# Soft-routed experts on one core: the last set of weight sums cut in two halves, and the first product's additions at other places

## The chip, the cores and the metric

The kernel runs on one core of a Trainium2 chip. The metric is the device time of one execution in microseconds; the median of three runs is given, and one further execution was taken with the hardware profiler. TensorE (PE) multiplies, VectorE (DVE) and ScalarE (ACT) compute, GpSimd (POOL), SyncE (SP) and ACT issue DMAs, each from an ordered queue of its own.

## The reference

Every token passes through all eight experts, and the results are added with the softmax of the router's logits as weights. There are 16 × 512 tokens of 512 values, eight matrices of 512 × 2048, and the output is 8192 × 2048 in float32.

```python
logits_max = np.max(router_logits, axis=-1, keepdims=True)
probs = np.exp(router_logits - logits_max)
probs = probs / np.sum(probs, axis=-1, keepdims=True)
output = np.zeros((batch, seq, expert_hidden), dtype=np.float32)
for e in range(n_experts):
    expert_out = np.matmul(x, expert_weights[e])
    output += probs[:, :, e:e+1] * expert_out
```

## The kernel before, in words

Since the weight of an expert is a factor per token, the sum over experts is one large matrix product: the tokens' rows, scaled by each expert's probability and set side by side, times the eight expert matrices set on top of each other. The kernel computes it by a scheme of Strassen and Winograd with seven products for eight, twice nested. The outer seven are called P1 to P7. The blocks of the left side are two expert halves by the even and odd 256-token blocks; a number q from 0 to 15 names a pair of such blocks ("row pair"). The blocks of the right side are two expert halves by two column halves, called 11, 12, 21 and 22, 22 being the lower right one. The output blocks are C11 and so on.

Inside a product of one row pair there are again seven steps, each of eight matmuls of 128 × 512 into one PSUM bank. Such a step is a "slot", and the kernel's own clock puts it at 1.73 us (`SLOT`). Most stages hold two row pairs and thus 14 slots. The stages run in this order: P1 (0 to 6), P2 (7 to 14), P5 and P6 mixed (15 to 31, where `k5` = 15 is the first and `k6` = 31 the last), P7 and P4 in turn (32 to 47, `k7` = 32; P7 is in the even stages, P4 in the odd ones), and P3 (48 to 56, `k3` = 48). P4 and P3 take their first steps in thirds (`by_thirds`), so their pieces are smaller.

The order of the program is written by hand. `at(stage, slot, make)` hangs an action on a slot, and `slots_after(stage, slot, n)` counts n slots on across stages. DVE's work that isn't tied to a matmul goes into a queue by `later(cost, make)`, and `slack()` takes tasks from it whenever the kernel's own clock has DVE ahead of PE. `flush(task)` empties that queue up to a task. All subtractions and additions on DVE are issued by `tt` (line 110), all DMAs of POOL by `pool` (line 124), those of SP by `sp` (line 121), whole weight blocks by ACT in `fetch_w` (line 167), and all matmuls by `mm` (line 133).

The buffers that matter here: `w`, 15 weight blocks of 1 MB; `h`, 12 places of 256 KB for results on their way to the output ("result places"), where also the rows that a product is added onto are fetched (`h<-kept`, rows of P1 put aside in DRAM, and `h<-out_dram`, rows of the output written earlier); `u`, one single buffer of 512 KB, for a temporary left side, for weight pieces, and in P4's stages for four small sums (`room_u`). A place is used again when the program's semaphores say that its last reader, often a DMA, is done.

The right sides of P4 and P3 are differences of weight blocks, and they are made while earlier products run. P4's are made in quarters (`by_parts`: first quarter at stage 17, slot 4, then every 38 slots). P3's are made in eighths by `by_eighths`: an eighth loads four pieces of 128 KB of block 22 (`u<-wd`), makes four differences in place on DVE through `sums_in_place`, and stores each (`wd<-u`). Before it begins it flushes the last eighth's tasks. All eight were hung at stage 17, slot 8 + 17j. From stage 46 on, ACT fetches the finished blocks for P3, 1 MB each (`turnover`).

P1 is needed in several output blocks. For ten of the row pairs it is added to C11 by DMAs of POOL that accumulate from DRAM to DRAM (`add_kept`, `out_dram<-kept` in the profile): four of 256 KB for each pair, forty in all. They were hung from stage 35 on, one every four slots.

At stage 28 ACT loads pieces into `u` for P7's first difference (`ahead_part`).

Of the kernel before, what the change touches and what calls it, by code (L numbers as in the profile page):

```python
# [31 lines left out]
def kernel(  # L32
# [8 lines left out]
    P = 128  # L41
    f16 = mybir.dt.float16
# [7 lines left out]
    C = H // P  # L50
    HE = E // 2
    NB = 512
# [24 lines left out]
    def h_tile(shape, dtype):  # L77
        return hpool.tile(shape, dtype, name="h", tag="h")
# [19 lines left out]
    def note(i):  # L98
        last[i.ins.engine] = i.ins
        if ordered[0]:  # L100
            tc.keep_in_program_order(i)
# [21 lines left out]
    def pool(o, i, **how):  # L123
        note(nc.gpsimd.dma_start(out=o, in_=i, **how))  # L124
# [15 lines left out]
    def new_u():  # L140
        return zpool.tile([P, K8, HQ], f16, name="u", tag="u", bufs=1)
# [18 lines left out]
    def kept_w(what, kn):  # L160
        if (what, kn) not in stored:
            stored[what, kn] = dram.tile([P, K8, NB], f16, name="wd")
        return stored[what, kn]
# [209 lines left out]
    def flush(task):  # L373
        while task is not None and not task.done:
            queue.popleft().run()
# [340 lines left out]
    def at(stage, slot, make):  # L716
        hooks.setdefault((stage, slot), []).append(make)

    def add(*products):
        stages.append(products)  # L720
        return len(stages) - 1
# [43 lines left out]
    def product(r, q, **how):  # L765
        left, loads = left_of(r, q)
        lefts[r, q] = left
        p = None
        if r == 1:
            def sink(tn, o):  # L770
                pool(kept_rows(q)(tn), o)
            p = Product(right[1], left, sink)
        elif r == 2:
            if q >= ON_BASE or q in WITH_KEPT:
                bases[2, q] = Base(kept_rows(q))
            p = Product(right[2], left, to_out(q, 0, 0), bases.get((2, q)))
        elif r == 5:
            bases[6, q] = m1 = Base(kept_rows(q))
            m1.task = {}

            p = Product(right[5], left, to_out(q, 1, 0))
        elif r == 6:
            m1 = bases[6, q]

            def base(tn):
                need(m1.task[tn])
                return m1.t[tn]
            p = Product(right[6], left, to_out(q, 0, 1), base)
        elif r == 7:
            base = products[6, q].o.__getitem__  # L790
            if q < KEPT_Z:
                base = bases[7, q] = Base(lambda tn: out_rows(q, 0, 1, tn))
            p = Product(right[7], left, to_out(q, 1, 1), base)
        elif r == 4:
            p = Product(right[4], left, to_out(q, 1, 0, accum_op=ADD), products[7, q].o.__getitem__)
        else:
            p = Product(right[3], left, to_out(q, 0, 1, accum_op=ADD), **how)
        p.loads = loads
        products[r, q] = p
        return p  # L800
# [198 lines left out]
    k5 = add(product(5, 0), product(5, 1))  # L999
# [5 lines left out]
    k7 = k6 + 1  # L1005
# [4 lines left out]
    k3 = add(product(3, 0))  # L1010
    for q in ((1, 2), (3, 14), *zip(range(4, 14, 2), range(5, 14, 2))):
        add(*(product(3, i) for i in q))
    end = add(product(3, 15))
# [28 lines left out]
    for n, q in enumerate(ORDER_7[1:], 1):  # L1042
        stage = k7 + 2 * n
# [71 lines left out]
    for i, (kn, e) in enumerate((kn, e) for kn in (ODD, (0, 0), (1, 1), (1, 0)) for e in range(2)):  # L1115
        stage = ND + i - 2 if kn != ODD else 2 + 2 * i
# [4 lines left out]
    ORDER = ((0, 0), (0, 1), (1, 1), (1, 0))  # L1121
# [13 lines left out]
    def sums_in_place(part, b, r, cost):  # L1135

        def one(p, o, x, y):
            def make():
                tt(o, x, y, SUB)
                part(p, o)  # L1140
            return later(cost, make)
        one(5, b[0, 0], b[0, 1], b[0, 0])
        one(7, b[0, 1], b[1, 1], b[0, 1])
        one(6, b[1, 1], b[1, 1], b[0, 0])
        return one(4, b[1, 0], b[1, 0], b[1, 1])
# [13 lines left out]
    def slots_after(stage, slot, n):  # L1159
        slot += n  # L1160
        while slot >= 7 * len(stages[stage]):
            slot -= 7 * len(stages[stage])
            stage += 1
        return stage, slot

    def part_of(what, kn, chunks):
        return kept_w(what, kn)[:, chunks, :]
# [3 lines left out]
    def by_parts(stage, slot, every, r, load, between, when):  # L1171

        for j in range(4):
            b, chunks = {}, ds(2 * j, 2)

            def begin(b=b, j=j, chunks=chunks):
                flush(last_part[0])
                t = new_w()
                for i, kn in enumerate(ORDER):
                    b[kn] = t[:, ds(2 * i, 2), :]  # L1180
                    load(b[kn], kn, j, chunks)

            def go_on(b=b, chunks=chunks):
                for kn in b:
                    if kn != ODD:
                        between(b[kn], kn, chunks)

            def end(b=b, chunks=chunks):
                last_part[0] = sums_in_place(lambda p, o: pool(part_of((r, p), (0, 0), chunks), o), b, r, 0.69)
            at(*slots_after(stage, slot, j * every), begin)  # L1190
            if between is not None:
                at(*slots_after(stage, slot, j * every + when[0]), go_on)
            at(*slots_after(stage, slot, j * every + when[-1]), end)

    last_eighth = [None]

    def by_eighths(stage, slot, j):

        b, chunk = {}, ds(j, 1)

        def begin():
            flush(last_eighth[0])
            t = new_u().rearrange("p (i two) t -> p i (two t)", two=2)
            for i, kn in enumerate(ORDER):
                b[kn] = t[:, ds(i, 1), :]
                pool(b[kn], part_of("b22", kn, chunk))

        def end():
            last_eighth[0] = sums_in_place(lambda p, o: pool(part_of((3, p), (0, 0), chunk), o), b, 3, 0.42)
        at(*slots_after(stage, slot, 0), begin)  # L1210
        at(*slots_after(stage, slot, 9), end)

    def cast_part(q):
        def load(t, kn, j, chunks):
# [17 lines left out]
        later(0.69, make)  # L1232

    by_parts(k5 + 2, 4, 38, 4, load_p4, less_t2, (9, 20))
    for j in range(2 * C):
        by_eighths(k5 + 2, 8 + 17 * j, j)


    RAW = {1: (0, 0), 2: (1, 0), 3: (1, 1)}
# [99 lines left out]
    def add_kept(q, n, t):  # L1339
        pool(out_f[ds(2 * q * HQ + t * HP, HP), ds(n * NB, NB)], kept[q][n, ds(t * HP, HP), :], accum_op=ADD)  # L1340

    for n, q in enumerate(q for q in range(ON_BASE) if q not in WITH_KEPT):
        for i in range(4):
            at(*slots_after(k7 + 3, 0, 16 * n + 4 * i), lambda q=q, i=i: add_kept(q, i // 2, i % 2))

    finish = products[3, 15]
    finish.base = Base(lambda tn: out_rows(15, 0, 1, tn))
# [90 lines left out]
```

## Time and profile before

| what | us |
|---|---|
| median of 3 runs | 1383.88 |
| lowest and highest | 1382.93, 1389.23 |
| the profiled execution | 1386.03 |
| its span on the core | 1384.3 |
| mean granted TensorE clock in it | 0.991 of full speed |

In the profile's rows, a line such as "518.84 4.97 PE L133 MATMUL ps<-w,z ... x16 [3.96 <-DVE h L110]" reads: at 518.84 us after the span's start a run of 16 matmuls of line 133 began, which took 4.97 us; ahead of it PE was idle for 3.96 us, and what came last was DVE's work on a tile `h` at line 110. Tiles go by their names in the program without numbers; `wd` are blocks of weights in DRAM, `ps` and `pt` banks of PSUM, `z`, `d` and `u` left sides. "POOLq" and "SPq" are the DMA issues of these engines. In a table of DMA issues the last column is the median time from issue to landing.

### The profile page before, as it was taken

The page shows a single profiled execution, that of the slowest core. Times are in us where ns is not written, and L with a number is a line of the kernel's source. Part 1 is how long each engine was busy: PE and PEld are TensorE (multiplying, and loading weights), DVE is VectorE, ACT ScalarE, POOL GpSimd, SP SyncE. Part 2 cuts the span into 40 slices and gives each one's busy share as a digit, 9 for nine tenths or more (in the row PEclk, how much of TensorE's full clock was granted, in tenths as well). Part 3 has the DMA queues.
Part 4 walks back from the last instruction along what each step waited for, and adds up shares of the span by engine and source line. Part 5 has one row for each costly group of instructions (what it writes and reads, how often), then busy time and mean ns, then how long its engine had stood idle before and what let it go on. Part 6 is the DMA issues. An engine that isn't in the chain of part 4 may idle for free.

```text
span 1384.3 us, 19408 instructions
## 1 busy us (share of the span) xinstructions
PE 1353.9 (98%) x7062; PEld 689.7 (50%) x7062; DVE 1156.1 (84%) x1474; ACT 274.1 (20%) x573; POOL 437.1 (32%) x683
## 2 busy tenths in 40 slices
PE   9999999999999989999898999999999999899998
PEld 4556655555544434444343444554555455456554
DVE  7878898888898878878668789889888987898886
ACT  3233332222211111111101100110110011133331
POOL 3223332233233254435321212333433341223232
PEclk9999999999999999999998999999999999999999
DMA  9899979998999999999999888899999999999986
GB/s 184 245 213 249 274 220 254 297 286 260 305 302 275 279 293 309 289 310 301 274 266 315 291 303 198 203 250 200 261 261 217 230 254 320 314 282 230 218 128 121
DMA packets 187601, 355.71 MB, mean 257 GB/s; under 512 B 53104, under 2 KB 82032, under 8 KB 182640
## 3 DMA queue, kind: packets, MB, share of 16 engines
q0 software_dynamic: 88032, 185.12, 58.4%
q1 hardware_dynamic: 95728, 144.05, 34.8%
q10 hardware_dynamic: 3744, 25.30, 5.2%
q8 instruction: 55, 0.90, 0.3%
q14 instruction: 42, 0.34, 0.1%
HBM read 210.53 MB, written 176.36 MB: 279 GB/s over the span
## 4 chain that ended last, share of the span: by engine, by line
PE 41%; issue 7%; DMA 5%; POOL 1%; DVE 0%; POOLq 0%; ACT 0%; DVEq 0%
PE ps L133 32%; PE pt L133 8%; DMA out_dram<-h 2%; POOL out_dram L124 1%; DMA wd<-w 1%; DMA xs<-in_x_dram 1%; DMA wd<-u 1%; DVE h L110 0%; POOL u L124 0%; DVE ps L110 0%; DVE z L110 0%; DVE w L110 0%; POOL xs L124 0%; POOLq L124 0%; ACT h L1375 0%
## 5 line engine op out<-in xcount | busy, mean ns | idle before, releaser
L133 PE MATMUL ps<-w,z 128*128 128x512 f16 (+1 forms) x3784 | 823.6, 374 | 19.7 <-DVE h L110 13.1
L133 PEld LDWEIGHTS <-z 128*128 128x128 f16 x5256 | 515.1, 98 | 570.2 <-issue 23.3
L124 POOL DMA_DIRECT2D out_dram<-h x380 | 250.9, 667 | 650.2 <-ACT h L674 229.2
L133 PE MATMUL pt<-w,z 128*128 128x512 f16 (+1 forms) x1444 | 286.3, 343 | 0.0
L110 DVE TENSOR_TENSOR h<-ps,h 128x512 f32<-128x512 f32 x298 | 202.6, 687 | 73.1 <-PE ps L133 53.3
L110 DVE TENSOR_TENSOR z<-xT,pT 128x2048 f16<-128x2048 f16 x192 | 232.0, 1218 | 0.8 <-DMA xT<-xs 0.8
L133 PE MATMUL ps<-w,d 128*128 128x512 f16 x880 | 202.4, 382 | 4.4 <-DVE ps L110 4.4
L661 ACT COPY h<-ps 128x512 f32<-128x512 f32 x102 | 59.9, 587 | 400.3 <-PE ps L133 363.3
L133 PEld LDWEIGHTS <-d 128*128 128x128 f16 x880 | 86.7, 99 | 104.1 <-issue 8.3
L110 DVE TENSOR_TENSOR z<-z,d 128x2048 f16<-128x2048 f16 x110 | 131.9, 1218 | 0.0
L110 DVE TENSOR_TENSOR w<-w 128x1024 f16<-128x1024 f16 (+2 forms) x98 | 105.9, 1100 | 7.5 <-DMA wd<-w 5.9
L674 ACT COPY h<-ps 128x512 f32<-128x512 f32 x54 | 31.7, 587 | 283.0 <-PE ps L133 259.8
L110 DVE TENSOR_TENSOR h<-pt,h 128x512 f32<-128x512 f32 x95 | 64.9, 687 | 24.3 <-PE pt L133 22.2
L110 DVE TENSOR_TENSOR h<-h 128x512 f32<-128x512 f32 (+2 forms) x69 | 45.3, 678 | 36.4 <-DMA h<-kept 33.1
L110 DVE TENSOR_TENSOR d<-z 128x1024 f16<-128x1024 f16 x110 | 73.5, 685 | 0.7
L110 DVE TENSOR_TENSOR ps<-ps,h 128x256 f32<-128x256 f32 (+1 forms) x84 | 50.4, 603 | 19.4 <-PE ps L133 14.8
L657 ACT COPY h<-ps 128x512 f32<-128x512 f32 x89 | 49.9, 599 | 76.6 <-PE ps L133 55.7
L124 POOL DMA_DIRECT2D kept<-h x56 | 30.6, 548 | 87.6 <-DVE h L110 48.2
L110 DVE TENSOR_TENSOR z<-z 128x2048 f16<-128x2048 f16 (+1 forms) x52 | 50.5, 978 | 1.6
L653 ACT COPY ps<-ps 128x512 f32<-128x512 f32 x47 | 26.8, 570 | 112.8 <-PE ps L133 76.5
L124 POOL DMA_DIRECT2D wd<-u x40 | 21.7, 544 | 61.9 <-DVE u L110 46.5
L124 POOL DMA_DIRECT2D out_dram<-kept x40 | 40.3, 1080 | 2.7 <-issue 1.3
(100 smaller groups left out, 705.8 us busy)
## 6 DMA issues: line engine op xcount, KB each, us to landing
out_dram<-h POOLq DMA_DIRECT2D x380, 256.0 KB, 7.8
z<-z SPq DMA_DIRECT2D x56, 512.0 KB, 10.0
pT<-p_dram SPq DMA_DIRECT2D x94, 256.0 KB, 8.0
w<-wd ACTq DMA_DIRECT2D x23, 1024.0 KB, 9.9
h<-kept SPq DMA_DIRECT2D x88, 256.0 KB, 7.8
w<-in_expert_weights_dram POOLq DMA_DIRECT2D x33, 512.0 KB, 11.3
xT<-x SPq DMA_DIRECT2D x64, 256.0 KB, 7.8
h<-out_dram SPq DMA_DIRECT2D x60, 256.0 KB, 10.1
```

The source lines that it names most:

```text
L110: dve(nc.vector.tensor_tensor(out=o, in0=a, in1=b, op=op))
L124: note(nc.gpsimd.dma_start(out=o, in_=i, **how))
L133: note(nc.tensor.matmul(ps, z, w, start=start, stop=stop, skip_group_check=True))
L653: act(nc.scalar.copy(self.banks["b"], x))
L657: act(nc.scalar.copy(o[tn], q if p == 5 else x))
L661: act(nc.scalar.copy(o[TN[p]], b if p == 2 else x))
L674: act(nc.scalar.copy(o[tn], b))
```

## The change

The eight eighths of P3's sums are split. The first four stay amid P6 and P5 in `u`, but begin at stage 17, slot 24, and are 38 slots apart instead of 17. The other four are hung at slot 5 of the stages 34, 36, 38 and 40, which are P7's, and use two of the twelve result places instead of `u`. The sums of an eighth are queued 8 slots after its loads, not 9.

P1's additions to C11 begin at stage 34 instead of 35, at 4.5 slots from one to the next instead of 4. Eight of the ten row pairs are done so (up to stage 43, slot 13); the additions for the last two (q = 12 and 13) are hung in P3's stages 53 and 54.

The number of instructions and DMAs of each engine is the same. In the order of the built program PE's instructions are unmoved, and SP's too; DVE's and POOL's are the same ones in another order. Some waits of SP are others, since result places are taken over from other users: in the P4 stages that follow an eighth in P7, the first fetch of output rows (`h<-out_dram`) waits for that eighth's stores.

```diff
@@ -1194,21 +1194,28 @@
-    def by_eighths(stage, slot, j):
+    def room_of_u():
+        t = new_u().rearrange("p (i two) t -> p i (two t)", two=2)
+        return [t[:, ds(i, 1), :] for i in range(4)]
+
+    def room_of_h():
+        t = [h_tile([P, 2, NB], f16) for i in range(2)]
+        return [t[i // 2][:, ds(i % 2, 1), :] for i in range(4)]
+
+    def by_eighths(stage, slot, j, room):
 
         b, chunk = {}, ds(j, 1)
 
         def begin():
             flush(last_eighth[0])
-            t = new_u().rearrange("p (i two) t -> p i (two t)", two=2)
-            for i, kn in enumerate(ORDER):
-                b[kn] = t[:, ds(i, 1), :]
-                pool(b[kn], part_of("b22", kn, chunk))
+            for kn, t in zip(ORDER, room()):
+                b[kn] = t
+                pool(t, part_of("b22", kn, chunk))
 
         def end():
             last_eighth[0] = sums_in_place(lambda p, o: pool(part_of((3, p), (0, 0), chunk), o), b, 3, 0.42)
         at(*slots_after(stage, slot, 0), begin)
-        at(*slots_after(stage, slot, 9), end)
+        at(*slots_after(stage, slot, 8), end)
@@ -1232,8 +1239,9 @@
     by_parts(k5 + 2, 4, 38, 4, load_p4, less_t2, (9, 20))
-    for j in range(2 * C):
-        by_eighths(k5 + 2, 8 + 17 * j, j)
+    for j in range(C):
+        by_eighths(k5 + 2, 24 + 38 * j, j, room_of_u)
+        by_eighths(k7 + 2 + 2 * j, 5, C + j, room_of_h)
@@ -1341,7 +1349,8 @@
     for n, q in enumerate(q for q in range(ON_BASE) if q not in WITH_KEPT):
         for i in range(4):
-            at(*slots_after(k7 + 3, 0, 16 * n + 4 * i), lambda q=q, i=i: add_kept(q, i // 2, i % 2))
+            where = (k7 + 2, 18 * n + 4.5 * i) if n < 8 else (k3 + 5, 14 * (n - 8) + 3.5 * i)
+            at(*slots_after(where[0], 0, int(where[1])), lambda q=q, i=i: add_kept(q, i // 2, i % 2))
```

## The prediction, made before the result was known

> **What bounds the kernel now.** I read the page's head first, then the table of windows, then TensorE's rows that begin after a wait, and last what each of those waits was for.
>
> ```profile
> span 1384.3 us, 19408 instructions
> PE 1353.9 (98%) x7062; PEld 689.7 (50%) x7062; DVE 1156.1 (84%) x1474; ACT 274.1 (20%) x573; POOL 437.1 (32%) x683
> ```
>
> TensorE (PE) sets the time: it is busy for 1353.9 of 1384.3 us. The change leaves every matmul, so it can only touch the 30 us in which PE waits, and what PE loses to a lower clock after a wait. The windows show where that is. The columns are the stretch, its length, the busy time of PE, PEld, DVE, ACT and POOL (with instructions), the granted clock, the DMA share and GB/s.
>
> ```profile
> 430.00:700.00 270.00, 258.59 (x1179) 115.95 (x1178) 219.89 (x292) 36.95 (x64) 111.68 (x200) 0.98 1.06 291
> 700.00:800.00 100.00, 90.87 (x413) 40.66 (x412) 73.75 (x88) 11.39 (x20) 18.02 (x33) 0.95 0.93 288
> 880.00:1140.00 260.00, 260.00 (x1367) 133.43 (x1365) 222.17 (x286) 29.73 (x69) 95.68 (x127) 1.00 1.05 239
> 1140.00:1200.00 60.00, 56.42 (x283) 27.85 (x282) 47.59 (x63) 7.33 (x16) 14.43 (x20) 0.97 1.03 327
> 1290.00:1345.00 55.00, 55.00 (x312) 30.38 (x311) 46.28 (x60) 17.05 (x37) 17.99 (x21) 1.00 0.87 144
> ```
>
> PE loses 11.4 us in 430–700 (P6 and P5, where all eight eighths now lie), 9.1 us in 700–800 (the end of P6 and P5), 3.6 us at P3's start, and nothing in 880–1140 (P7 and P4, where the change puts work) or in 1290–1345 (P3's end). One stall after another, from the timeline; in brackets is the wait ahead of the row.
>
> ```profile
> 518.84 4.97 PE L133 MATMUL ps<-w,z 128*128 128x512 f16 x16 [3.96 <-DVE h L110]
> 523.65 3.62 PE L133 MATMUL pt<-w,z 128*128 128x512 f16 x16
> 621.84 1.89 PE L133 MATMUL ps<-w,z 128*128 128x512 f16 x8 [2.98 <-ACT h L657]
> 690.52 6.15 PE L133 MATMUL ps<-w,d 128*128 128x512 f16 x16 [4.22 <-DVE ps L110]
> 733.22 5.30 PE L133 MATMUL ps<-w,z 128*128 128x512 f16 x16 [8.91 <-DVE h L110]
> 1180.67 13.79 PE L133 MATMUL ps<-w,z 128*128 128x512 f16 x56 [3.58 <-DVE z L110]
> ```
>
> Sixteen undisturbed matmuls take 3.62 us, so a wait costs itself and what the next row is longer by: 518 costs 3.96 + 1.35 = 5.31, 621 costs 2.98, 690 costs 4.22 + 2.53 = 6.75, 733 costs 8.91 + 1.68 = 10.59. That is 25.6 us in P6 and P5. P3's start: 56 × 3.62 / 16 = 12.67, so 3.58 + 1.12 = 4.7 us. What stands behind each:
>
> ```profile
> 514.50 0.69 DVE L110 TENSOR_TENSOR h<-h 128x512 f32<-128x512 f32 x1 [6.84 <-DMA h<-kept]
> 513.60 0.54 POOL L124 DMA_DIRECT2D u<-wd  x1 [2.76 <-DMA out_dram<-h]
> 610.88 2.14 POOL L124 DMA_DIRECT2D u<-wd  x4 [5.30 <-DMA wd<-u]
> 621.20 0.59 ACT L657 COPY h<-ps 128x512 f32<-128x512 f32 x1 [10.43 <-DMA out_dram<-h]
> 689.17 0.69 DVE L110 TENSOR_TENSOR w<-w 128x1024 f16<-128x1024 f16 x1 [1.18 <-DMA wd<-w]
> 689.60 0.54 POOL L124 DMA_DIRECT2D wd<-u  x1 [5.90 <-DMA wd<-w]
> 714.48 11.40 SPq L121 DMA_DIRECT2D pT<-p_dram  x2
> 728.88 0.69 DVE L110 TENSOR_TENSOR h<-h 128x512 f32<-128x512 f32 x1 [10.73 <-DMA h<-kept]
> 1178.79 0.69 DVE L110 TENSOR_TENSOR h<-ps,h 128x512 f32<-128x512 f32 x1 [2.66 <-DMA out_dram<-h]
> ```
>
> All five are late DMAs: P1's rows for P6 (518, 733), a result's store that must free its place (621, 1180), a store of P4's sums (690). Two queues make them late. POOL issues in order, and an issue of the built program waits until the one eight before it has landed: at 513.60 a `u<-wd` load waits for an unrelated `out_dram<-h`. And u is one buffer, so an eighth's loads wait until the last eighth's stores have landed (610.88). SP's queue is the other: it stood 11.40 us at 714.48, ahead of the rows that 728.88 waits for.
>
> **The change, part by part.** First the eighths. Each is four loads and four stores of POOL and four subtractions; eight of them are 64 issues, all in 430–700 now.
>
> ```profile
> L124 POOL DMA_DIRECT2D u<-wd x32 | 17.2, 543 | 45.4 <-DMA wd<-u 32.3 <-issue 7.9 <-DMA out_dram<-h 5.1
> L124 POOL DMA_DIRECT2D u<-wd x32: 537/539/577, 443.8 to 668.6; - x32
> L110 DVE TENSOR_TENSOR u<-u x32: 414/420/427, 473.1 to 679.3; 128x512 f16<-128x512 f16 x32
> out_dram<-h POOLq DMA_DIRECT2D x81, 256.0 KB, 8.1
> u<-wd POOLq DMA_DIRECT2D x32, 128.0 KB, 7.5
> wd<-u POOLq DMA_DIRECT2D x32, 128.0 KB, 7.0
> ```
>
> The first row says that POOL stood idle 32.3 us in this window ahead of `u<-wd` loads, for stores of the eighth before; the second puts the first load, at slot 8, at 443.8 us. After the change an eighth begins every 38 products instead of every 17, at the kernel's own 1.73 us each 65.7 us instead of 29.4, so that wait goes whole. Thirty-two of the window's 200 POOL issues leave: eight in flight over 270 us allow 8 × 270 / 200 = 10.8 us from issue to landing now and 8 × 270 / 168 = 12.9 us after, against medians of 7.0 to 8.1 us in these rows. DVE loses 16 × 0.42 = 6.7 us here. POOL's and DVE's totals don't change.
>
> What that gives, stall by stall. 621: the issues behind `u<-wd` are no longer 5.30 us late, which is more than PE's loss; −2.98. 518: the first eighth moves to slot 24, 443.8 + 16 × 1.73 = 471.5 us, and the second to 537; the first now took 30 us to its first subtraction (473.1), so near 505 it is over and none runs until 537; POOL's wait at 513.60 and the traffic of eight DMAs beside P1's rows go; −5.31, at worst 0. 690: DVE's `w<-w` waits for stores queued on POOL among the eight stores of the last two eighths; after, the fourth eighth's four loads come at 443.8 + 130 × 1.73 = 668.7, with the two stalls ahead near 676 of the old clock, and its stores after 690, up to 705, so some crowd stays: I take −6 of 6.75, at worst 0. 733: here the eighths are nearly over, and what is late is SP's own issue (714.48), behind transposes and next to ACT's weight loads, which stay. Fewer DMAs and a stream that runs some 14 us ahead help, but the row names nothing that the change removes; I take two thirds, −7, with ends 0 and −10.59. Sum for P6 and P5: −21.3, from −9 (518 and 733 stay) to −25.6. ACT's own load into u near 710 waits for the fourth eighth's stores, some 3 us later by their place in POOL's order; ACT waited 10.43 us at 621 for a loss of 2.98, so this is 0, at worst 3.
>
> Then the four eighths in P7 (stages 34, 36, 38, 40, slot 5), in two of the twelve result places. These rows are of 880–1140, and two first accumulations of P7, one pair of stages apart:
>
> ```profile
> out_dram<-h POOLq DMA_DIRECT2D x88, 256.0 KB, 10.2
> h<-out_dram SPq DMA_DIRECT2D x46, 256.0 KB, 10.4
> out_dram<-kept POOLq DMA_DIRECT2D x39, 256.0 KB, 12.4
> 885.31 19.69 SPq L121 DMA_DIRECT2D h<-out_dram  x7
> 904.18 0.69 DVE L110 TENSOR_TENSOR ps<-ps,h 128x512 f32<-128x512 f32 x1
> 951.73 0.69 DVE L110 TENSOR_TENSOR ps<-ps,h 128x512 f32<-128x512 f32 x1
> ```
>
> A pair (P7, P4) lasts 951.73 − 904.18 = 47.55 us. Now it holds 16 results and 7 additions of P1, 23 issues or so (127 in 260 us); eight in flight allow 8 × 260 / 127 = 16.4 us, and the landings are (88 × 10.2 + 39 × 12.4) / 127 = 10.9 us. After, the additions are 4 in 18 products, 6.2 in a pair's 28, so a pair has 16 + 6.2 + 8 = 30.2 issues and allows 8 × 47.55 / 30.2 = 12.6 us. The eighth adds 1 MB to 239 GB/s × 47.55 us = 11.4 MB; 10.9 us scaled by that are 11.8. It fits with 0.8 us to spare on the mean, so sometimes it won't. Second, in the changed order SP's first fetch of out rows in each following P4 stage waits for the eighth's stores, whose places it takes over; before it ran free at 885.31. The sums are queued at slot 13, some 24 us into the P7 stage, the stores land 10 to 12 us later, near 888 in this pair; with 10.4 us for the rows that is about 899 against a use at 904.18. Five microseconds are left, and DVE's queue can take them. No row shows this price. The nearest is P3's start, 4.7 us, where DVE waited for result stores in the same way; the ends are 0 and 4.7 for each of four pairs, thus 0 to 18.8. I take 3 for each, +12, since both margins are thin.
>
> Last, P1's additions. The same 40 issues, four products sooner and a little wider apart: in P7 nothing by themselves. Eight of them leave 1090–1143 for P3's end, where PE lost nothing, DMA moved 144 GB/s in the windows' last row and stores landed thus:
>
> ```profile
> out_dram<-h POOLq DMA_DIRECT2D x21, 256.0 KB, 6.3
> ```
>
> 0 there. Before P3's start fewer of them are in flight, but what is late there is mostly due to these (1140–1200):
>
> ```profile
> w<-wd ACTq DMA_DIRECT2D x7, 1024.0 KB, 11.1
> out_dram<-h POOLq DMA_DIRECT2D x18, 256.0 KB, 14.5
> ```
>
> Seven 1 MB loads stay where they are; I take −2 of 4.7, ends 0 and −4.7. The sum is −21.3 + 12 − 2 = −11.3 us. The profiled execution took 1386.03 us, 1.7 beyond its span and 2.15 above the median of the runs, 1383.88; it would become 1374.7, and the median 1372.6. I call 0.5%, 6.9 us, the least that a measurement tells from no change: faster is below 1377.0, slower above 1390.8.
>
> The Trainium skill, "DMA: Bandwidth & Descriptors", section "Anatomy of one DMA — SWDGE (gpsimd) path", gives about 2.0 us plus bytes / 436e3 for one such DMA. By it, an estimate, 128 KB take 2.3 us and 256 KB 2.6 us, so that eight in flight never bind and the P7 term is 0. The rows above disagree, with 7.0 to 12.4 us, on a DMA share above 1.0.
>
> **The rivals.** *P7 stays clear.* Both margins hold; the +12 falls to 0 and the sum is −21.3 − 2 = −23.3, 1360.6 us; with every stall gone as well −25.6 − 4.7 = −30.3, 1353.6. For it: 260.00 busy of 260.00, and 0.8 and 5 us of room. Against: DMA share 1.05 there already. This is also what the page's short landings would give. 0.20.
>
> *The stalls stay and the price comes.* 518 and 733 are P1's rows arriving late through SP's queue, and the eighths are only near. Then −9 + 12 − 2 = +1, 1384.9; with half of P7's price 1378.9. For it: at 728.88 the wait is on SP, and the fourth eighth still falls there. 0.18.
>
> *P7 becomes the bound.* Once landings pass 12.6 us in the pairs with an eighth, POOL falls behind: result stores land late, DVE and ACT wait for places, and the fetches behind them make the next P7 late. Then both the P4 start and the next P7 start in each of four pairs cost 4.7 us doubled by the backlog they pass on: 4 × 9.4 = +37.6, with −21.3 and −2 +14.3, 1398.2. For it: landings of 14.5 us in 1140–1200 with fewer POOL issues (20 in 60 us). Against: there seven 1 MB loads ran. 0.16.
>
> **How the numbers follow.** The forecast, 1372.6, has 0.46; its own range is 1363 (P7 term halved, −6, and 733 wholly gone, −3.6) to 1380 (733 stays, +7). Of that 0.06 lies above 1377. Faster: 0.40 + 0.20 = 0.60. Same: 0.06 + 0.16 of the second rival, and 0.01 of the third where its price halves, 0.23. Slower: 0.15 of the third and 0.02 of the second, 0.17. The range, 1357 to 1391, leaves out most of the third rival (0.13) and the best ends of the first (0.05).
>
> **What would show it.** Right: no `u<-wd` idle for `wd<-u` on POOL; no PE rows with waits near 518, 621 and 690; a smaller one near 733; small new PE waits at P7's and P4's starts between 880 and 1050, each ended by a store or out rows; 1290–1345 still wholly busy. Wrong: the wait near 733 whole, 860–1050 wholly busy, or PE waits of 8 us and more there with POOL waiting for `wd<-h` or `out_dram<-kept`.

## The result, and the profile after

| kernel | us, median | lowest to highest | runs |
|---|---|---|---|
| before | 1382.93 | 1379.19 to 1389.23 | 5 |
| changed | 1363.77 | 1362.99 to 1372.44 | 5 |

The ratio is 0.987 (95% interval 0.9828 to 0.9911), so the change takes 12 to 24 us off, 18 by the ratio and 19.2 between the medians. The forecast was 11.3 us off, 1372.6, with a range of 1357 to 1391.

The head of the page after and the same windows as before, with the same columns:

```profile
span 1362.1 us, 19445 instructions
PE 1346.8 (99%) x7062; PEld 687.8 (50%) x7062; DVE 1156.3 (85%) x1474; ACT 274.8 (20%) x573; POOL 437.9 (32%) x683
```

```profile
430.00:700.00 270.00, 270.00 (x1252) 122.41 (x1251) 229.51 (x293) 39.10 (x67) 99.84 (x177) 1.00 1.07 298
700.00:800.00 100.00, 99.78 (x464) 45.15 (x462) 83.58 (x97) 11.69 (x20) 17.69 (x33) 1.00 0.88 303
880.00:1140.00 260.00, 252.38 (x1303) 127.23 (x1301) 218.66 (x289) 27.50 (x62) 92.97 (x132) 1.00 0.98 238
1140.00:1200.00 60.00, 59.56 (x333) 32.33 (x331) 51.91 (x67) 14.07 (x31) 14.86 (x19) 1.00 1.05 337
1290.00:1345.00 55.00, 55.00 (x311) 30.34 (x310) 46.55 (x58) 16.91 (x37) 21.44 (x26) 1.00 0.91 153
```

In this execution P6 and P5 (430–800) have no loss left but 0.22 us. P3's start, 3.58 us before, has no wait; the 0.44 us of the fourth window lie later, inside P3. P7 and P4, which had lost nothing, lose 260 − 252.38 = 7.62 us. P3's end, with the eight moved additions, stays full. The clock is 1.00 everywhere, so the new waits cost no more than themselves. Here they are (PE's rows):

```profile
905.40 0.60 PE L133 MATMUL pt<-w,z 128*128 128x256 f16 x4 [1.37 <-DVE ps L110]
954.71 0.60 PE L133 MATMUL pt<-w,z 128*128 128x256 f16 x4 [1.60 <-DVE ps L110]
967.19 5.34 PE L133 MATMUL ps<-w,z 128*128 128x512 f16 x24 [1.34 <-DVE h L110]
1006.00 0.60 PE L133 MATMUL pt<-w,z 128*128 128x256 f16 x4 [1.15 <-DVE ps L110]
1066.01 12.25 PE L133 MATMUL ps<-w,z 128*128 128x512 f16 x56 [1.11 <-DVE h L110]
```

These are all in P4's stages: at 905, 954 and 1006 in their first steps, which are taken in thirds, at 967 and 1066 in the later ones. (The four rows left out have waits of 0.17 to 0.45 us.) DVE's and POOL's rows show two causes.

```profile
886.29 1.14 POOL L124 DMA_DIRECT2D h<-wd  x2 [5.90 <-DMA out_dram<-h]
893.83 0.54 POOL L124 DMA_DIRECT2D out_dram<-h  x1 [4.98 <-DMA out_dram<-h]
948.88 0.56 POOL L124 DMA_DIRECT2D out_dram<-h  x1 [2.43 <-DMA out_dram<-h]
950.30 1.60 POOL L124 DMA_DIRECT2D out_dram<-h  x3 [0.86 <-DMA h<-wd]
901.46 0.43 DVE L110 TENSOR_TENSOR h<-h 128x512 f16<-128x512 f16 x1 [2.79 <-DMA h<-wd]
960.66 0.69 DVE L110 TENSOR_TENSOR h<-ps,h 128x512 f32<-128x512 f32 x1 [3.20 <-DMA out_dram<-h]
```

POOL's loads of the eighth stood 5.90 us for a result place whose store had not landed. They arrive late, and DVE, in its order, waits 2.79 us for them at 901.46 with P4's first additions behind. Later results are held up on POOL, where a store's issue waits for the landing of the DMA issued eight before it (4.98 us at 893.83; in the next pair of stages 2.43 and 0.86 us, the last for a load of the eighth). So their places come free late: the store issued at 950.30 landed at 960.63, and DVE, waiting for its place, stood 3.20 us at 960.66.

On POOL, the wait ahead of `u<-wd` is gone as forecast: 45.4 us of idle time, 32.3 of it for `wd<-u`, have become 2.7 with none.

```profile
L124 POOL DMA_DIRECT2D u<-wd x16 | 8.6, 541 | 2.7 <-DMA wd<-w 1.5 <-DMA out_dram<-h 1.2
```

### The profile page after: what moved, and what is told of

Same layout as the page of the kernel before. It is cut to its first block, busy times and chain, and to the rows that moved or that the text cites. A ratio compares the mean times of both kernels' runs of the same rounds, so it can differ in the third digit from the quotient of the medians.

```text
span 1362.1 us, 19445 instructions
## 1 busy us (share of the span) xinstructions
PE 1346.8 (99%) x7062; PEld 687.8 (50%) x7062; DVE 1156.3 (85%) x1474; ACT 274.8 (20%) x573; POOL 437.9 (32%) x683
## 4 chain that ended last, share of the span: by engine, by line
PE 86%; DMA 12%; DVE 1%; issue 1%; POOL 0%; ACT 0%; DVEq 0%; POOLq 0%; SPq 0%
PE ps L133 66%; PE pt L133 20%; DMA out_dram<-h 6%; DMA out_dram<-kept 1%; DMA w<-z 1%; DMA h<-wd 1%; DMA h<-out_dram 1%; DMA w<-wd 1%; DVE h L110 1%; DMA w<-in_expert_weights_dram 1%; POOL out_dram L124 0%; DVE z L110 0%; DVE u L110 0%; DVE ps L110 0%; POOL w L124 0%
## 5 line engine op out<-in xcount | busy, mean ns | idle before, releaser
L110 DVE TENSOR_TENSOR h<-h 128x512 f32<-128x512 f32 (+3 forms) x85 | 51.9, 628 | 8.9 <-DMA h<-wd 8.3
L133 PEld LDWEIGHTS <-h 128*128 128x128 f16 x384 | 37.6, 98 | 4.3
```

The lines of the kernel that those rows point to most:

```text
L110: dve(nc.vector.tensor_tensor(out=o, in0=a, in1=b, op=op))
L133: note(nc.tensor.matmul(ps, z, w, start=start, stop=stop, skip_group_check=True))
```

## The experiments

Each ratio is against runs of the kernel before on the same chip. Those medians were 1380.47 us for the first four experiments, 1384.75 for the next four and 1384.38 for the last four. The profile of an experiment is one execution, and not always a typical one; each group of four ran on a chip of its own.

**The eighths alone, and the additions alone.** The first keeps the change's eighths and has `add_kept` as before; the second the other way round.

```diff
-            where = (k7 + 2, 18 * n + 4.5 * i) if n < 8 else (k3 + 5, 14 * (n - 8) + 3.5 * i)
-            at(*slots_after(where[0], 0, int(where[1])), lambda q=q, i=i: add_kept(q, i // 2, i % 2))
+            at(*slots_after(k7 + 3, 0, 16 * n + 4 * i), lambda q=q, i=i: add_kept(q, i // 2, i % 2))
```

> The eighths as in the change, P1's additions as before (from stage 35, every four slots, all in P7 and P4). Theory A (each part pays where it lies: the eighths clear P6 and P5, and the additions that left 1090 to 1143 clear P3's start): P6 and P5 stay free of waits, P7 and P4 lose 8 to 12 us where the change lost 7.6 in 880 to 1140, since a pair of stages now has 31 POOL issues instead of 30.2, and P3's start loses its 4.7 us again: 1368 to 1373. Rival B (P3's start was cleared by the shift of everything ahead of it, the additions are worth nothing): 1363 to 1366, with no wait at P3's start.

> P1's additions as in the change, all eight eighths amid P6 and P5 at a pitch of 17 as before. Theory A: the waits in P6 and P5 stay (25.6 us in the profile of before), P7 and P4 stay without waits, P3's start loses 0 instead of 4.7: 4 to 5 us less than before, 1378. Rival B: P3's start still loses about 4.7: 1383.

Measured: eighths alone 1369.97 us (0.9935, 0.99 to 0.9971), additions alone 1372.63 us (0.9952, 0.992 to 0.9983). PE's row at P3's start with the eighths alone, and the window around it with the additions alone:

```profile
1180.15 13.95 PE L133 MATMUL ps<-w,z 128*128 128x512 f16 x56 [4.60 <-DVE z L110]
```

```profile
880.00:1140.00 260.00, 260.00 (x1345) 131.50 (x1343) 222.22 (x285) 27.50 (x62) 87.48 (x115) 1.00 1.00 230
1140.00:1200.00 60.00, 60.00 (x335) 32.61 (x333) 51.96 (x71) 11.29 (x26) 14.77 (x20) 1.00 0.99 321
```

Theory A holds for P3's start: it loses 4.60 us, and a lower clock, with the additions as before, and nothing once eight additions are out of the way, with 16.7 us of waits still in P6 and P5. Rival B, that the shift of everything ahead cleared it, isn't refuted by these two alone, for in the profile of the eighths alone P3 began only 0.5 us sooner than before. Two later runs refute it. In the kernel before with ACT's loads later, whose additions stay, P3 begins at 1174.15 us after a wait of 4.53. With eight eighths 19 slots apart and the additions moved the same matmul, by count, begins at 1174.17, without a wait:

```profile
1174.15 13.85 PE L133 MATMUL ps<-w,z 128*128 128x512 f16 x56 [4.53 <-DVE z L110]
```

```profile
1140.00:1200.00 60.00, 60.00 (x322) 31.42 (x321) 52.64 (x69) 10.29 (x23) 15.21 (x21) 1.00 0.98 317
```

Theory A's other half, P6 and P5 free of waits, failed in this execution of the eighths alone: PE lost 2.5 us between 430 and 700 and 9.6 between 700 and 800. By the ratios the parts are worth 9.0 and 6.6 us, together 15.6, beside 18.0 for both; each has an interval of some 5 us either way, so they add up as far as can be told.

**The change without its eighths in P7.** One line goes, so half of the work on P3's differences isn't done, and P3 multiplies raw blocks in place of all four differences. What it computes is thus another product, with the same matmuls and the same loads of 1 MB.

```diff
-        by_eighths(k7 + 2 + 2 * j, 5, C + j, room_of_h)
...
-                right[r].w[p] = fetch_w((r, p), (0, 0))
+                right[r].w[p] = fetch_w(*(("b22", {5: (0, 0), 6: (1, 1), 7: (1, 0), 4: (0, 0)}[p]) if r == 3 else ((r, p), (0, 0))))
```

> The change without its four eighths in P7 (half of P3's weight differences are not made, and P3 multiplies by raw blocks in their place; the same matmuls and the same 1 MB loads). Theory A (the 7.6 us lost in 880 to 1140 come from these eighths): P7 and P4 have no waits, about 1356. Rival C (they come from the additions, four slots sooner and beside P7's rows): the waits stay, 1362 to 1364.

Measured 1354.37 us (0.9835, 0.9793 to 0.9876), all runs within 3.1 us, and P7 and P4 without a wait:

```profile
880.00:1140.00 260.00, 260.00 (x1354) 132.25 (x1352) 221.81 (x287) 28.58 (x65) 82.21 (x112) 1.00 0.99 235
```

So these four eighths are the whole price in P7: 7.6 us between the profiles, 9.4 between the medians, which are of two groups of runs, and 5 by the ratios. Rival C falls.

**Number or pitch in P6 and P5.** First the change's four eighths in `u`, but 17 slots apart and beginning at slot 8 as before, not 24; then all eight in `u`, 19 apart, with none in P7.

```diff
-        by_eighths(k5 + 2, 24 + 38 * j, j, room_of_u)
+        by_eighths(k5 + 2, 8 + 17 * j, j, room_of_u)
```

> The change, but its first four eighths begin at stage 17, slot 8, and are 17 slots apart as before, so they are over by stage 22. Theory S (the pitch counts: an eighth's loads wait for the last one's stores on POOL and hold up what is behind): POOL's idle time ahead of u<-wd for wd<-u comes back at some 6 us for each gap, and with it the wait of PE near 518 us (5.3 us): 1369, the later ones stay away. Rival N (the number counts: 32 fewer issues and 4 MB less in this stretch clear it): no wait of PE in P6 and P5, 1364.

```diff
-    for j in range(C):
-        by_eighths(k5 + 2, 24 + 38 * j, j, room_of_u)
-        by_eighths(k7 + 2 + 2 * j, 5, C + j, room_of_h)
+    for j in range(2 * C):
+        by_eighths(k5 + 2, 5 + 19 * j, j, room_of_u)
```

> All eight eighths amid P6 and P5 in u again, from stage 17, slot 5, but 19 slots apart instead of 17; P1's additions as in the change. Theory S (pitch): 19 slots are 32.9 us and an eighth takes about 30 us with landing, so most of POOL's wait for wd<-u returns, and with four more eighths the stalls of P6 and P5 too: 1368 to 1375, P7 without waits. Rival G (before sat just beyond an edge, two slots are enough): 1355 to 1360, better than the change.

Measured 1373.74 us (0.9957, 0.9923 to 0.9992) and 1373.51 us (0.9954, 0.9914 to 0.9994). Of the first kernel POOL's group, two of PE's rows and two of DVE's, then of the second POOL's group and a row of PE:

```profile
L124 POOL DMA_DIRECT2D u<-wd x16 | 8.6, 544 | 18.0 <-DMA wd<-u 12.4 <-DMA out_dram<-h 4.8 <-DMA wd<-w 0.8
526.58 9.60 PE L133 MATMUL ps<-w,z 128*128 128x512 f16 x32 [4.74 <-DVE h L110]
599.44 0.91 PE L133 MATMUL ps<-w,z 128*128 128x512 f16 x3 [4.55 <-DVE h L110]
```

```profile
525.00 0.93 DVE L110 TENSOR_TENSOR u<-u 128x512 f16<-128x512 f16 x2 [8.93 <-DMA u<-wd]
595.10 0.69 DVE L110 TENSOR_TENSOR h<-h 128x512 f32<-128x512 f32 x1 [7.44 <-DMA xs<-in_x_dram]
```

```profile
L124 POOL DMA_DIRECT2D u<-wd x32 | 17.4, 549 | 41.3 <-DMA wd<-u 19.8 <-DMA out_dram<-h 13.8 <-DMA w<-in_expert_weights_dram 4.4
729.87 5.78 PE L133 MATMUL ps<-w,z 128*128 128x512 f16 x16 [15.06 <-DVE h L110]
```

The four eighths at the old pitch cost 8 to 10 us more than at 38 slots by the medians (1363.77 and, below, 1365.38; 10 to 12 by the ratios), with the same number of DMAs in P6 and P5. So their spacing counts, as theory S says, or the earlier slot at which they begin; no run parts these two. The wait at 526 is of theory S's kind: POOL's issue of these loads had waited for the last eighth's stores, they took 15.0 us to land, and DVE stood 8.93 us for them. But it isn't the wait near 518 come back, for it lies 32 matmuls later in the program, and at 514.50 in the profile of before DVE stood for P1's rows.

The row at 599 doesn't fit: the last of these four eighths stored at 570, and PE lost 4.55 us all the same. DVE's row ahead of it names a load of x, and P1's rows landed in the same 0.1 us, so it isn't an eighth that was late there. Nor is the wait near 518 a fixture of the kernel before: the additions alone and the kernel before with later loads are the same program up to there, and in their profiles PE doesn't wait near 518. It waits elsewhere, from 539 on, and loses 9.2 and 12.1 us between 430 and 700, beside 11.4 in that of before.

Two slots more of pitch for all eight (rival G) are no cure. The 15.06 us near 730 come after the last eighth's stores (707.7): there SP's transposes began at 703.82, ACT's 1 MB load followed at 704.49, and SP's next issue stood 13.47 us, which belongs to the next question.

**The wait near 733.** That place lost 10.6 us in the profile of before and 0 in that of the change. A second measurement of the changed kernel, and the eighths alone, whose program up to there is the same as the change's, lost other amounts:

> The changed kernel itself, beside the three others of this call on one chip. 1363 to 1366, with 6 to 9 us of waits of PE between 880 and 1140 and none in P6 and P5. If P6 and P5 are clear only by luck of one execution, some runs lie 10 us higher, as one of its first five did (1372.44).

Measured 1365.38 us (0.9885, 0.9811 to 0.996), 1361.01 to 1367.93. PE's rows of this one, and of the eighths alone, which was profiled in the slowest of its ten runs, 1385.63 (that kernel's others lay from 1367.30 to 1374.21):

```profile
711.48 5.30 PE L133 MATMUL ps<-w,z 128*128 128x512 f16 x16 [2.96 <-DVE h L110]
```

```profile
720.42 4.91 PE L133 MATMUL ps<-w,z 128*128 128x512 f16 x16 [9.37 <-DVE h L110]
```

So the same instructions lose 0, 4.6 or 10.7 us there from one execution to another. What differs in these is how long SP's two transposes take, with ACT's 1 MB load at their side. The tables of DMA issues around them, for the eighths alone and for the change (694 to 702 and 686 to 690 us; the last column is the median to landing):

```profile
w<-wd ACTq DMA_DIRECT2D x1, 1024.0 KB, 17.5
xT<-xs SPq DMA_TRANSPOSE x2, 12.3
```

```profile
xT<-xs SPq DMA_TRANSPOSE x2, 4.4
```

With the eighths alone the load was issued at 697.43, under 3 us after the transposes began, and SP's next issue then stood 10.04 us:

```profile
700.49 10.04 SPq L121 DMA_DIRECT2D pT<-p_dram  x2
```

In the change's profile the load came 7 us after the transposes began. The second measurement lies between: the load was 2.6 us behind and the transposes took 6.1 us. To test this, ACT's loads were moved, in the change and in the kernel before:

```diff
-    at(k6 - 3, 1, begin_ahead)
-    for e, load, go in ((0, (k6 - 3, 2), (k6 - 3, 9)), (1, (k6 - 3, 13), (k6 - 2, 6))):
+    at(k6 - 3, 6, begin_ahead)
+    for e, load, go in ((0, (k6 - 3, 7), (k6 - 3, 13)), (1, (k6 - 2, 3), (k6 - 2, 9))):
```

> The change, with ACT's three loads for P7's first difference (1 MB, and twice 512 KB into u) four to five slots later in stages 28 and 29. Theory T: the wait near 710 to 733, which this same program had in one execution and not in the next, is a race between SP's transposes and ACT's 1 MB load; when the load comes second by under 2 us the transposes land after 13 to 16 us instead of 3.5 to 5, SP's next issue waits for them, and P1's rows come late. With the load 8 us later it never meets them: no such wait, 1361 to 1363 in nearly every run. Rival U (the load has no part in it; SP is simply late behind x's own load): runs as spread as the change's, 1361 to 1368.

> The kernel before with only those ACT loads four to five slots later. Theory T: the wait at 733 of the profile of before (10.6 us with its lower clock) goes without any change of the eighths, and the other waits in P6 and P5 and at P3's start stay: 7 to 10 us less than before. Rival V (there SP is late through the eighths' crowding, as the prediction supposed for two thirds): under 3 us less.

Measured 1360.93 us (0.9842, 0.9804 to 0.9879), its four runs from 1360.89 to 1361.29; and 1377.10 us (0.9954, 0.9924 to 0.9983), 7.3 below the median of before. Of the second kernel the window and the transposes:

```profile
700.00:800.00 100.00, 97.26 (x451) 43.97 (x450) 80.69 (x97) 12.26 (x21) 19.84 (x37) 1.00 0.98 305
xT<-xs SPq DMA_TRANSPOSE x2, 6.8
```

PE lost 9.1 us in this window in the profile of before and loses 2.7 here, without any change of the eighths, as theory T says; P3's start and some 12 us between 430 and 700 stayed.

All the profiles say the same. In six the load was issued within 3 us of the first of the two transposes: in five of these PE lost 7.2 to 15.1 us of waiting at this place, in one 2.96. In the other eight it came 7 us or more after it, and PE lost nothing there. A lag of 2 to 3 us between transposes and load is not enough by itself (6.1 us in one execution, 12.3 in another), so what else decides is open.

Three things temper this. Moved later, the load can meet the next pair of transposes: in this second kernel they began at 725.29, 1.2 us behind it, and took some 17 us, and PE waited 2.52 us at 744.70. Transposes are also slow with no load of ACT near: two took 16.4 us in the profile of before, at 676, amid the eighths' DMAs. And of the profiles with the load in its old place all three with eight eighths in P6 and P5 had the meeting, but only three of the seven with four; that is too few to say whether the change makes it rarer.

**The price in P7.** One kernel issues the P7 eighths' DMAs on SP; two others take additions out of P7. The one with five pairs in P7 has ACT's loads later as well, and so has a repeat of the one with six.

```diff
-    def by_eighths(stage, slot, j, room):
+    def by_eighths(stage, slot, j, room, send=pool):
...
-                pool(t, part_of("b22", kn, chunk))
+                send(t, part_of("b22", kn, chunk))
...
-        by_eighths(k7 + 2 + 2 * j, 5, C + j, room_of_h)
+        by_eighths(k7 + 2 + 2 * j, 5, C + j, room_of_h, sp)
```

> The change, with the loads and stores of its four eighths in P7 issued by SP instead of POOL; everything else as it is. Theory D (the price in P7 is POOL's: 30.2 issues in a pair with eight in flight): POOL is back at 22.2 issues in a pair, PE's 7.6 us there fall to under 3, 1357. Rival E (the price is the traffic and the two result places, whichever queue issues): it stays, 1362 to 1366; and if SP, now waiting for places and for DVE's sums ahead of P7's rows, becomes late itself, over 1372.

```diff
-            where = (k7 + 2, 18 * n + 4.5 * i) if n < 8 else (k3 + 5, 14 * (n - 8) + 3.5 * i)
+            where = (k7 + 2, 24 * n + 6 * i) if n < 6 else (k3 + 4, 14 * (n - 6) + 3.5 * i)
```

> The change, but six row pairs' additions from stage 34 at six slots from one to the next, and four pairs' in stages 52 to 55 (16 additions in P3 instead of 8). Theory D: a pair has 16 + 4.7 + 8 = 28.7 issues, which allows 13.3 us to landing instead of 12.6, and 1.5 additions less of traffic; PE's loss between 880 and 1140 halves, 1359 to 1361, nothing is lost in P3. Rival F (the price lies in the eighth's own wait for places): 1363 to 1365. If P3's end has no room for 16, over 1366 with waits after 1230.

> The change with six row pairs' additions from stage 34 at six slots from one to the next, four pairs' in stages 52 to 55, and ACT's loads later as well. If both help apart from each other: 1355 to 1358 with a spread of 3 us; PE loses about 3 us between 880 and 1140 and nothing in P6 and P5. If the load's place does nothing, the same as without it, 1357 in the median and single runs over 1362.

```diff
-            where = (k7 + 2, 18 * n + 4.5 * i) if n < 8 else (k3 + 5, 14 * (n - 8) + 3.5 * i)
+            where = (k7 + 2, 28 * n + 7 * i) if n < 5 else (k3 + 3, 14 * (n - 5) + 3.5 * i)
```

> As the last, but five row pairs' additions from stage 34 at seven slots from one to the next, and five pairs' (20 additions) in stages 51 to 55. Theory D: a pair has 16 + 4 + 8 = 28 issues, which allows 13.6 us; PE's loss between 880 and 1140 falls to 1 to 2 us: 1354 to 1356. If P3 has no room for 20 (DMA share 1.05 from 1200 to 1290), waits come in 1230 to 1320: over 1358.

Measured: by SP 1368.97 us (0.9895, 0.9804 to 0.9986); fewer additions 1357.29 (0.9836, 0.9762 to 0.991); fewer and later 1357.44 (0.9823, 0.9788 to 0.9859); half and later 1356.71 (0.9825, 0.9782 to 0.9869). The window of P7 and P4 in the first, second and fourth of these:

```profile
880.00:1140.00 260.00, 254.05 (x1310) 128.00 (x1309) 219.81 (x289) 27.47 (x62) 86.49 (x114) 1.00 1.00 237
```

```profile
880.00:1140.00 260.00, 257.18 (x1329) 129.91 (x1328) 223.55 (x295) 27.49 (x62) 90.28 (x130) 1.00 0.98 237
```

```profile
880.00:1140.00 260.00, 257.56 (x1331) 130.00 (x1329) 223.42 (x295) 27.51 (x62) 86.72 (x126) 1.00 0.97 235
```

On SP the loss is 5.95 us, as much as in the change's second profile (254.04 of 260 busy), with POOL down to 114 instructions from 132. Theory D asked for under 3, so as it was put it falls. This doesn't clear the queues, though. With SP issuing, most of PE's waits for result places went, and SP's own rows came late instead: SP's issues, too, stood for the eighth's loads to land (13.9 us in all), and DVE waited for rows that SP fetches ahead of PE's 0.72 us at 957. So what a queue with room to spare would pay is open. What stays are the loads, which DVE waits for. These are DVE's row and PE's behind it, with SP issuing:

```profile
1019.99 0.42 DVE L110 TENSOR_TENSOR h<-h 128x512 f16<-128x512 f16 x1 [2.03 <-DMA h<-wd]
1023.33 0.60 PE L133 MATMUL pt<-w,z 128*128 128x256 f16 x4 [2.93 <-DVE ps L110]
```

That kernel's profile, the slowest of its four runs, also had waits between 588 and 725 us, where its program is the change's.

Fewer additions in P7 do help. The change's P7 and P4 lose 5.4 to 7.6 us in three profiles (the change twice, and with ACT's loads later), the three kernels with fewer additions 2.4 to 3.9; the medians are 4 to 9 us lower. Theory D had POOL's count of issues for the reason; that there is less traffic beside the eighths would do as well, and these runs don't tell. P3's end took 16 and 20 additions without a wait. On top of fewer additions ACT's later loads brought nothing in the median, against what was expected: 1357.29 and 1357.44. Nor did they end the spread: the six runs of fewer and later lie from 1354.80 to 1364.58, those of half and later from 1355.47 to 1369.09, and the profile of the former had another wait, 3.71 us at 663.85. The medians of the three versions near 1357 all lie below the change's, though their intervals overlap; between them these runs can't choose.

One caution holds for all of this. Nine profiles have the change's first four eighths, 38 slots apart. In six of them PE waits for nothing between 430 and 700, and in three it loses 2.5 to 6.3 us there (the eighths alone, P7 by SP, fewer and later). The three with eight eighths 17 slots apart lose 9 to 12 us, the one 19 apart 4.5. So the new pitch clears this stretch in most executions, not in all.

## Why the prediction was right, and where its steps were off

The sign, the place of each gain and the place of the loss were right, and the time lay in the range. Between the two profiled executions the span fell by 22.2 us: about 25.6 in P6 and P5 (the prediction's four waits) and 4.7 at P3's start, less 7.6 in P7 and P4 and 0.44 in P3. The median fell by 19.2, since the profiled execution of before, 1386.03, was itself 3.1 us above the later median.

*518, 621, 690 (−5.31, −2.98, −6).* Gone whole in the change's two profiles, and the "crowd" that was to leave 0.75 us at 690 did not cost anything. That the pitch and the single buffer make loads late is what the four eighths at 17 slots show, at another place. For the single waits the cause is only argued: those near 620 and 690 stand in all three profiles with eight eighths at 17 slots, but the one at 518 in one of the three, so that the 5.31 us came out whole is partly luck.

*733 (−7 of 10.6).* Wrong in reason, and in size right by luck alone: against the profile of before this place gained 10.6 us in the change's first profile, 6 in its second, and nothing in that of the eighths alone. The prediction said that the row "names nothing that the change removes" and then took two thirds for fewer DMAs and an earlier stream. The runs show a meeting of SP's transposes with ACT's 1 MB load, which the same program sees in some executions and not in others; the kernel before is rid of that wait, too, when the load is moved. It is no steady gain of the eighths.

*P7 (+12).* Mis-sized: 7.6 us in the first profile, 6.0 in the second, and 5 to 9.4 by ratios and medians. Of the two margins the second held: SP's fetches did wait for the eighth's stores, but no P7 start waited. The first overran: the loads issued at 886 took over 14 us to land, and POOL's issues stood for the DMA eight before. How much of the price that was is open, since SP as the issuer paid as much in other waits. One mechanism was missing: DVE takes its work in order, and an eighth's sums that wait for their loads hold up the first additions of P4.

*P3's start (−2 of 4.7).* Mis-sized. The prediction held the seven 1 MB loads to be the cause and the additions to be minor. With the additions alone moved PE lost nothing there; with the eighths alone it lost 4.60 us and more. The loads were in both, so they are not enough by themselves; whether they are needed no run tests. All fourteen profiles agree: the three with the additions as before lose 3.6 to 4.6 us at P3's start, the eleven others nothing.

The four terms that were off by size, 690, 733, P7 and P3's start (0.75, 3.6, 4.4 and 2.7 us), were all off to the same side, which is why the span fell by twice the forecast's 11.3 us.

Of the rivals, "P7 becomes the bound" is out, since no wait there was over 1.6 us in the change's profile and over 2.43 in its second. "P7 stays clear" came nearer to the time than the forecast did, but it is out by the price. "The stalls stay and the price comes" is out for the change's own profiles; the longest execution of the eighths alone, 1385.63 us, is much like it, with the wait near 733 whole and the price paid.

By the fit in the Trainium skill, "DMA: Bandwidth & Descriptors", section "Anatomy of one DMA — SWDGE (gpsimd) path", one DMA of 128 KB takes 2.3 us, an estimate. This trace does not agree: the eighths' loads took a median of 12.6 us.

```profile
h<-wd POOLq DMA_DIRECT2D x12, 128.0 KB, 12.6
```

## What to carry to other kernels

Where one buffer is filled, used and stored in turn, space its uses by the whole trip, with the landing of the stores, or the queue that fills it stands still for everyone behind; here four uses 38 slots apart, and begun 16 slots later, were worth some 10 us over 17 apart. Before crediting a wait's end to a change, look at the same stretch in several executions, and ask whether two transfers only happened to meet. When work moves to a stage that had no waits, cost it by the engine that takes it in order as well as by the queue that issues it.

## What was not expected of the hardware

Two transposes and a 1 MB load on another queue, near one another, took 12.3 and 17.5 us to land, where the transposes took 4.4 us when the load came 7 us later.

Whether a wait of 2 to 3 us costs clock can't be told from its length. The 2.51 us at 665 with SP issuing and the 2.96 at 711 in the change's second profile were each followed by sixteen matmuls in 5.30 us instead of 3.62; the 2.52 us at 745 in the kernel before with later loads by sixteen in 3.61, and the 2.98 at 621 in the profile of before by eight in 1.89, the same as undisturbed ones. The granted clock in these traces is either 1.00 or 0.50. In the profile of before it was 0.50 from 518.21 for 3.41 us, from 688.87 for 6.83 and from 726.42 for 10.24, which are one, two and three times 3.41, and the three starts, too, lie whole multiples of 3.41 us apart (50 and 11). By that grid the wait at 665 lay 2.2 us within one step, while the one at 621 fell on two steps, with 1.7 and 1.2 us. That the share of a step spent waiting decides is read from these few cases, and no run varied it.
